# A two-layer conditioned trunk on one core: every engine's order computed in the kernel, and a first block in new rounds

## The chip, the core and the metric

The kernel runs on one core of one Trainium2 chip. A core has five engines that run side by side, each with its own queue of instructions that starts them in order: TensorE (PE in the profile; its weight loads are PEld) multiplies matrices, VectorE (DVE) and ScalarE (ACT) work on elements, GpSimd (POOL) does a few odd jobs, and SyncE (SP) issues most transfers. Data comes from device memory by DMA into the on-chip buffer SBUF; TensorE writes its results into PSUM, which has eight banks of 128 x 512 numbers. An engine waits for another by semaphores. The metric is the device time of one execution in microseconds (us), median of several runs.

## What is computed

One sequence of 256 positions, width 1024, two layers. Each layer is a half-step SwiGLU feed-forward, an attention, and another half-step feed-forward. Every sublayer first normalises x (RMS), then scales and shifts it with vectors that come from the condition c (adaLN), and multiplies its result by a gate that also comes from c:

```python
c_act = silu(c)
for layer in range(2):
    mods = c_act @ ada_w[layer] + ada_b[layer]
    sh1, sc1, g1, sh2, sc2, g2, sh3, sc3, g3 = split(mods, 9)
    h = rms_norm(x, norm_g[layer, 0]) * (1 + sc1) + sh1
    x = x + 0.5 * g1 * (silu(h @ w_gate) * (h @ w_up)) @ w_down
    ...
```

The attention of layer 0 ("MoBA") has 16 heads of 64, RMS-normalised q and k, a learned bias by bucketed distance, and a causal mask; with 256 positions it has a single block. Layer 1 ("MLA") projects x to small latents for q and for k and v, normalises, expands them to 16 heads, rotates a part of 32 (rope), and attends causally. All numbers are float32. 255 MB are read from device memory.

## The kernel before

**Products.** A float32 matrix is split into two parts of a shorter type, hi and lo (`split`: ScalarE copies to hi, VectorE subtracts to get lo, 128 x 1024 at a time). A product is then three matmuls, hi by hi, hi by lo and lo by hi (`mm3`, lines 394 to 396). Weights come in 0.5 to 1 MB transfers into a ring of three buffers (`rawp`, tile `raw`), in a fixed sequence (`wsrcs`, `wload`). A feed-forward makes a first block of 512 columns, then nine blocks of 256 columns of gate and up, then the down product.

**The adaLN vectors.** Eighteen vectors of 1024 are made beside the rest (`ada_vec`): eight slices of 128 x 1024 of ada_w come into a ring (tile `adaw`), and VectorE adds each, times c, to an accumulator (tile `acc`, line 211). The first step starts from a zeroed tile `bz` whose row 0 holds the bias, brought by a transfer from ScalarE's queue. TensorE then sums over partitions into a tile `adaps` (lines 222, 230 and 231).

**The first block.** It can't wait for the usual way. `first()` makes its shift and scale in four rounds of 256 columns: for each round two pairs of 0.5 MB transfers of ada_w and two of gate and up; VectorE's steps on 256 columns, shift and scale apart (`acc_step`); column sums on TensorE (`sums`, tile `at<-ones_r,acc`); `cols`; the modulated x (`shaped`, tile `z`); and then unsplit float32 products of z with the round's gate and up rows (`products`, tile `mm<-raw,z`; each is two records in the profile). Its order is written out by hand (`START`) and held by `in_turn` and `behind`, which queue each instruction behind the last of its engine. c comes as 1024 single numbers, one per element (`c_raw`).

**Side work.** The bias table of the MoBA attention is made during the first feed-forward (`bias_steps`: VectorE compares positions, tile `oh`, line 722; TensorE multiplies by table differences; ScalarE copies; the result goes to a DRAM tile `bias_d`). Rope tables and masks are made there too.

**Attention.** Per group of four heads: a projection into PSUM; square (line 698), sum (701), power on GpSimd (703) and scale give normalised q and k (`qn`, `kn`); TensorE transposes them (879, 1065); scores go into three PSUM banks (611); VectorE takes maxima, ScalarE exponentials (631), VectorE divides (637); TensorE transposes the probabilities (646) and multiplies by v (666). Between sublayers, x is normalised (`resid`, `stat`, `rstd_of`), transposed (442), modulated and split (`hh`, `hl`).

**Order.** Outside the first block the instructions are emitted by a clock of estimated matmul time: `later(us, fn)` emits fn when so much matmul work has been emitted, and a pace spreads the vectors. The tile scheduler then orders each engine's queue by this sequence. Transposes, scores and column sums share one ring of four PSUM banks (`ps_tr`); projections and products have the other four (`ps_mm`).

```python
ps_mm = ctx.enter_context(tc.tile_pool(name="ps_mm", bufs=4, space=PSUM))
ps_tr = ctx.enter_context(tc.tile_pool(name="ps_tr", bufs=4, space=PSUM))
```

Of the kernel before, what the change touches and what calls it, by code (L numbers as in the profile page):

```python
# [69 lines left out]


START = ("a10 a11 r0 a12 a13 y00 y01 q10 q11 y02 t00 y03 t01 a00 r1 b a01 a14 a02 y10 t02 a15 a03 "
         "y11 t03 y12 t10 y13 t11 t12 t13 a16 a04 a17 a05 a06 a07 s g").split()

BIAS_STEPS = [0, 0, 0, 3]
# [7 lines left out]
def bcast_row(ap, n, parts=P):  # L83
    return bass.AP(tensor=ap.tensor, offset=ap.offset, ap=[[0, parts], [1, n]])


@with_exitstack
def trunk(ctx: ExitStack, tc: tile.TileContext, a: dict, out: bass.AP):
# [11 lines left out]
    ps_tr = ctx.enter_context(tc.tile_pool(name="ps_tr", bufs=4, space=PSUM))  # L100
# [39 lines left out]
    def drain():  # L140
        while pend:
# [12 lines left out]
    bz = cp.tile([P, D], F32, name="bz")  # L154
    nc.vector.memset(bz, 0.0)
# [3 lines left out]
    c_raw = cp.tile([P, KD], F32, name="c_raw")  # L159
# [3 lines left out]
    nc.scalar.activation(cact, c_raw, AF.Silu)  # L163
# [10 lines left out]
    def split(src, n):  # L174
        hi = splitp.tile([P, n], F32R, tag="hi", name=nm("hi"))
        lo = splitp.tile([P, n], F32R, tag="lo", name=nm("lo"))
        in_turn(nc.scalar.activation, hi, src, AF.Copy, on="a")
        in_turn(nc.vector.tensor_tensor, lo, src, hi.bitcast(F32), op=ALU.subtract, on="v")
        return hi, lo

    chain = {}
    started = []

    @contextmanager
    def behind(*engines):

        with ExitStack() as es:
            for e in engines:
                if e in chain:
                    es.enter_context(tc.issue_after(chain[e].ins))  # L190
            yield

    def in_turn(fn, *args, on="p", **kw):

        if started:
            return fn(*args, **kw)  # L196
        with behind(on):
            chain[on] = fn(*args, **kw)  # L198
        return chain[on]

    def ada_vec(w, b, col, finish, rows):


        acc = adap.tile([P, D], F32, tag="acc", name=nm("acc"), bufs=1)
        nc.scalar.dma_start(bz[0:1, :], b[col:col + D].rearrange("(o n) -> o n", o=1))
        for k in range(KD):
            wt = adap.tile([P, D], F32, tag="adaw", name=nm("adaw"))
            with behind("s"):
                nc.sync.dma_start(wt, w[k * P:(k + 1) * P, col:col + D])
            with behind("v"):  # L210
                nc.vector.scalar_tensor_tensor(acc, wt, cact[:, k:k + 1], bz if k == 0 else acc,  # L211
                                               op0=ALU.mult, op1=ALU.add)
# [13 lines left out]
        def sums():  # L226
            for hh in range(2):
                pt = ps_tr.tile([P, 512], F32, tag="tr", name=nm("adaps"))
# [21 lines left out]
    def scale_col(ps, key, k0=0, n=KD):  # L250
        in_turn(nc.vector.scalar_tensor_tensor, col_slice(m_cols[:, 1, :], key, k0, n), ps, 1.0,
                col_slice(g_cols, key, k0, n), op0=ALU.add, op1=ALU.mult, on="v")
# [58 lines left out]
    def wsrcs():  # L311
        for layer in range(2):
            for idx in range(2):
                wg, wu, wd = (a[n][layer, idx] for n in ("ffn_w_gate", "ffn_w_up", "ffn_w_down"))
                if (layer, idx) == (0, 0):
                    for k0 in range(0, KD, 2):
                        yield [w[k0 * P:(k0 + 2) * P, :FB] for w in (wg, wu)], 4, FB
                else:
# [41 lines left out]
    def wload(src, kt, cols):  # L360
# [6 lines left out]
        for i, sr in enumerate(srcs):  # L367
            dst = rows[:, :, i * m:(i + 1) * m] if isinstance(src, tuple) else rows[:, i * n:(i + 1) * n, :]
            with behind("s"):
                ld = nc.sync.dma_start(dst, sr.rearrange("(k p) f -> p k f", p=P))  # L370
            if not started:
                chain["s"] = ld
# [35 lines left out]
    def split_evac(hi, lo, ps):  # L408
        in_turn(nc.scalar.activation, hi, ps, AF.Copy, on="a")
# [398 lines left out]
    def bias_step():  # L808

        if len(groups) < 2:  # L810
            next(side[0], None)
# [473 lines left out]
```

## Time and profile before

| | |
|---|---|
| median of 3 runs | 1063.77 us (1063.65 to 1065.18) |
| the profiled execution | 1067.16 us, span 1065.4 us |
| granted TensorE clock, mean | 0.998 |
| read from device memory | 255.33 MB, 244 GB/s over the span |
| instructions | 17278 |

The profile is one execution. Its span runs from the first to the last instruction on the core; "busy" is the time in which an engine has at least one instruction recorded as running, and the ends of matmuls are modelled. A group line names the line of the kernel, the engine, the operation, output and inputs with their shapes and the count, then busy time, the mean of one in ns, and the idle time of the engine ahead of it with what ended it. Many lines stand under a helper's line, so tiles are named where that matters.

### The profile page before, as it was taken

To read this page: it belongs to the slowest core of one execution; us is meant where nothing else is said; L and a number is where in the kernel's file an instruction comes from. 1 tells how busy PE (TensorE), PEld (TensorE's weight loads), DVE (VectorE), ACT (ScalarE), POOL (GpSimd) and SP (SyncE) were. 2 spreads that over 40 slices of the span, in tenths; PEclk is the share of its full clock that TensorE was granted. 3 is DMA by queue.
4 is the path that set the end of the run, shared out by engine and by line. 5 is a ranking of instruction groups with operands and counts; after the bars stand their busy time and mean duration, and the time that the engine had idled before them with its cause. 6 is when DMAs were issued, how large, how long until landed. Compare 5 with 4: busy or idle time off the path is not lost.

```text
span 1065.4 us, 17278 instructions
## 1 busy us (share of the span) xinstructions
PE 1020.8 (96%) x6663; PEld 899.3 (84%) x6663; DVE 810.9 (76%) x1244; ACT 578.6 (54%) x1048; POOL 70.1 (7%) x119
## 2 busy tenths in 40 slices
PE   4999999998999999999999999999988899999998
PEld 2499999886778789999887999988766778999986
DVE  5999977886875789889688888867778758755642
ACT  4364545357675765545348544533868777545531
POOL 4001000002121000000000000000043200000000
PEclk9999999999999999999999999999999999999999
DMA  9999987996845479989897997986354337665450
GB/s 311 322 304 287 376 288 278 335 318 206 310 162 170 139 236 345 337 293 332 295 313 227 328 329 251 318 303 205 117 162 142 119 119 236 223 204 187 161 177 20
DMA packets 166934, 260.65 MB, mean 245 GB/s; under 512 B 8030, under 2 KB 110214, under 8 KB 166852
## 3 DMA queue, kind: packets, MB, share of 16 engines
q1 hardware_dynamic: 164496, 254.70, 70.3%
q0 software_dynamic: 976, 3.37, 1.0%
q10 hardware_dynamic: 1380, 1.49, 0.5%
q8 instruction: 52, 0.85, 0.3%
q14 instruction: 30, 0.25, 0.1%
HBM read 255.33 MB, written 4.19 MB: 244 GB/s over the span
## 4 chain that ended last, share of the span: by engine, by line
PE 77%; DVE 10%; ACT 4%; DMA 4%; POOL 3%; issue 3%; SPq 0%; DVEq 0%; ACTq 0%; POOLq 0%
PE mm L394 23%; PE mm L396 23%; PE mm L395 23%; DVE lo L196 3%; POOL hr L703 3%; DMA adaw<-in_ada_w_dram 2%; PE mm L198 2%; ACT hi L196 1%; DVE oh L722 1%; PE adaps L222 1%; PE at L666 1%; PE at L611 1%; DVE acc L211 1%; DMA raw<-in_ffn_w_gate_dram 1%; ACT y L196 1%
## 5 line engine op out<-in xcount | busy, mean ns | idle before, releaser
L196 DVE TENSOR_TENSOR lo<-raw,hi 128x1024 fp32r<-128x1024 f32 (+2 forms) x316 | 374.3, 1199 | 80.2 <-ACT hi L196 79.3
L196 ACT ACTIVATE hi<-raw 128x1024 fp32r<-128x1024 f32 (+2 forms) x316 | 324.1, 1040 | 171.5 <-PE mm L396 103.6
L394 PE MATMUL mm<-hh,hi 128*128 128x256 f32 x1152 | 328.6, 285 | 0.0
L396 PE MATMUL mm<-hh,lo 128*128 128x256 f32 x1152 | 326.7, 284 | 0.5 <-DVE lo L196 0.5
L395 PE MATMUL mm<-hl,hi 128*128 128x256 f32 x1152 | 326.5, 283 | 0.0
L395 PEld LDWEIGHTS mm<-hl,hi 128*128 128x128 f32 x1152 | 221.7, 192 | 0.6 <-issue 0.2
L396 PEld LDWEIGHTS mm<-hh,lo 128*128 128x128 f32 x1152 | 221.6, 192 | 0.7 <-DVE lo L196 0.7
L394 PEld LDWEIGHTS mm<-hh,hi 128*128 128x128 f32 x1152 | 221.7, 192 | 0.6 <-issue 0.2
L211 DVE SCALAR_TENSOR_TENSOR acc<-adaw,cact,acc 128x1024 f32<-128x1024 f32 x126 | 162.8, 1292 | 20.6 <-DMA adaw<-in_ada_w_dram 16.2
L394 PE MATMUL mm<-hi,gh 128*128 128x512 f32 x352 | 138.0, 392 | 0.0
L395 PE MATMUL mm<-lo,gh 128*128 128x512 f32 x352 | 137.0, 389 | 0.0
L396 PE MATMUL mm<-hi,gl 128*128 128x512 f32 x352 | 137.0, 389 | 0.0
L394 PE MATMUL mm<-hi,hh 128*128 128x512 f32 (+1 forms) x240 | 96.7, 404 | 5.0 <-ACT hh L196 5.0
L396 PE MATMUL mm<-hi,hl 128*128 128x512 f32 (+1 forms) x240 | 94.0, 392 | 1.5 <-DVE hl L196 1.4
L395 PE MATMUL mm<-lo,hh 128*128 128x512 f32 (+1 forms) x240 | 93.4, 390 | 0.0
L560 ACT ACTIVATE g<-mm 128x256 f32<-128x256 f32 x72 | 27.3, 379 | 94.5 <-PE mm L396 94.5
L396 PEld LDWEIGHTS mm<-hi,gl 128*128 128x128 f32 x352 | 66.1, 188 | 13.8
L394 PEld LDWEIGHTS mm<-hi,gh 128*128 128x128 f32 x352 | 66.1, 188 | 13.2
L395 PEld LDWEIGHTS mm<-lo,gh 128*128 128x128 f32 x352 | 66.1, 188 | 13.1
L196 ACT ACTIVATE gh<-g 128x256 fp32r<-128x256 f32 x72 | 29.9, 416 | 69.6 <-DVE g L561 69.6
L394 PEld LDWEIGHTS mm<-hi,hh 128*128 128x128 f32 x240 | 45.1, 188 | 16.1 <-ACT hh L196 7.8
L396 PEld LDWEIGHTS mm<-hi,hl 128*128 128x128 f32 x240 | 45.1, 188 | 13.2 <-DVE hl L196 4.5
(222 smaller groups left out, 1114.8 us busy)
## 6 DMA issues: line engine op xcount, KB each, us to landing
adaw<-in_ada_w_dram SPq DMA_DIRECT2D x144, 512.0 KB, 6.8
raw<-in_ffn_w_gate_dram SPq DMA_DIRECT2D x42, 1024.0 KB, 7.3
raw<-in_ffn_w_up_dram SPq DMA_DIRECT2D x42, 1024.0 KB, 6.9
raw<-in_ffn_w_down_dram SPq DMA_DIRECT2D x40, 1024.0 KB, 6.6
raw<-in_moba_w_qkv_dram SPq DMA_DIRECT2D x16, 512.0 KB, 5.0
adaw<-in_kv_ada_w_dram SPq DMA_DIRECT2D x16, 512.0 KB, 5.6
raw<-in_ffn_w_down_dram SPq DMA_DIRECT2D x8, 512.0 KB, 3.6
raw<-in_moba_w_qkv_dram SPq DMA_DIRECT2D x4, 1024.0 KB
```

The lines of the kernel that those rows point to most:

```text
L196: return fn(*args, **kw)
L198: chain[on] = fn(*args, **kw)
L211: nc.vector.scalar_tensor_tensor(acc, wt, cact[:, k:k + 1], bz if k == 0 else acc, op0=ALU.mult, op1=ALU.add)
L222: nc.tensor.transpose(kslice(pt, j), kslice(acc, 4 * hh + j), ident)
L394: nc.tensor.matmul(ps, lh, rh, start=start, stop=False)
L395: nc.tensor.matmul(ps, lh, rl, start=False, stop=False)
L396: nc.tensor.matmul(ps, ll, rh, start=False, stop=stop)
L560: nc.scalar.activation(g, ps[:, 0], AF.Silu)
L611: nc.tensor.matmul(ps3[:, i, :], qTs(e, t), kTs(e, nk), start=bias is not None, stop=bias is not None or i == len(es) - 1)
L666: nc.tensor.matmul(po[i * DH:(i + 1) * DH, pr, t, :], vs(e, kb), pT[t, e, kb], start=kb == 0, stop=kb == t)
L703: nc.gpsimd.tensor_tensor(r, v2, mhalf[:, :nh], op=ALU.pow)
L722: return fn(*args, **kw)
```

## The change

**An order for every engine.** At the end of the kernel a new class reads all instructions emitted so far, works out who needs whom from the data each reads and writes, and from the rings of buffers, and places all instructions of the five engines in a modelled time. The model's durations are constants in the kernel. VectorE, ScalarE, GpSimd and SyncE take the ready instruction with the earliest latest time (`needs`); TensorE keeps the emitted order among those that are ready, but sums of adaLN vectors come first. This is repeated four times, each time with the last placement's times for TensorE, and the best is kept. Each engine's order is then chained, without semaphores: every instruction behind the one before it.

**The first block.** Five rounds of 128, 256, 256, 256 and 128 columns in place of four of 256. Shift and scale share an accumulator (512 columns a step); round 0 has no steps on VectorE, TensorE sums over ada_w itself (16 matmuls of one column). The hand-written order and its helpers are gone, and `wsrcs` leaves the first block's weights out.

**Smaller parts.** c comes as eight rows of 128, goes through Silu as rows, and is transposed by TensorE. An adaLN accumulator is zeroed by GpSimd, its row 0 is filled by a GpSimd transfer, and there are two of them; `bz` is gone. The column sums of the vectors get a PSUM bank of their own and the ring `ps_tr` has three. The bias steps and rope tables are not placed in the first 34 us.

```diff
+ROUNDS = (128, 256, 256, 256, 128)
+WAKE = 100.0
+SWITCH = 90.0
+RATE = 392.0
+FLIGHT = 8
+HELD = 34e3
+SOON = 300.0
+MARGIN = 400.0
+ROUND_OF_ORDER = 4
...
+def duration(i, aps):
...
+        elif dt == F32R:
+            c = max(256, cols) / 2.4 + 13.3
...
+class Order:
...
+    def needs(self, pe_time):
+        need = [1e12] * len(self.ins)
+        for k in range(len(self.ins) - 1, -1, -1):
+            then = [need[s] for s in self.succ[k]]
+            then += [need[self.uses[self.next_tile[t]][0]] for t in self.tiles_of[k] if t in self.next_tile]
+            d = min(then) - WAKE if then else 1e12
+            d -= 2200.0 + self.transfer(k) if self.dma[k] else self.cost[k][1]
+            if self.eng[k] == "PE":
+                d = min(d, pe_time[k])
+            need[k] = min([d] + [need[s] - 1.0 for s in self.after[k]])
...
+        def choose(e, t):
+            av = avail[e]
+            if e == "PE":
+                first = min(av)
+                old = [x for x in av if x[2] <= t - MARGIN]
+                x = min(old) if old else first
...
+            x = min(av)
+            for r, j in known[e]:
+                if r < t + min(self.cost[x[1]][0], SOON) and need[j] < x[0] - 500.0:
...
+    def apply(self):
+        info = mybir.DependencyInfo(mybir.DependencyClass.NoSync, mybir.DependencyReason.DATA)
+        for ks in self.work_out()[1].values():
+            for a, b in zip(ks, ks[1:]):
+                self.tc.add_manual_dep(self.ins[b], self.ins[a].name, info, reason="order")
...
-    ps_tr = ctx.enter_context(tc.tile_pool(name="ps_tr", bufs=4, space=PSUM))
+    ps_tr = ctx.enter_context(tc.tile_pool(name="ps_tr", bufs=3, space=PSUM))
+    ps_ada = ctx.enter_context(tc.tile_pool(name="ps_ada", bufs=1, space=PSUM))
...
-    nc.sync.dma_start(c_raw, a["c"].rearrange("o (k p) -> p (o k)", p=P),
-                      allow_slow_non_contiguous=True)
+    c_rows = tp.tile([P, 256], F32, tag="y", name="c_rows", bufs=4)[:KD, :P]
+    nc.sync.dma_start(c_rows, a["c"].rearrange("o (k p) -> (o k) p", p=P))
...
-        acc = adap.tile([P, D], F32, tag="acc", name=nm("acc"), bufs=1)
-        nc.scalar.dma_start(bz[0:1, :], b[col:col + D].rearrange("(o n) -> o n", o=1))
+        acc = adap.tile([P, D], F32, tag="acc", name=nm("acc"), bufs=2)
+        nc.gpsimd.memset(acc, 0.0)
+        nc.gpsimd.dma_start(acc[0:1, :], b[col:col + D].rearrange("(o n) -> o n", o=1))
...
-                pt = ps_tr.tile([P, 512], F32, tag="tr", name=nm("adaps"))
+                pt = ps_ada.tile([P, 512], F32, tag="ada", name=nm("adaps"))
...
     def bias_step():
 
         if len(groups) < 2:
-            next(side[0], None)
+            hold(lambda: next(side[0], None))
...
     def first():
...
+        nc.scalar.activation(c_rows, c_rows, AF.Silu)
+        pt = tr_tile()
+        nc.tensor.transpose(pt[:, :KD], c_rows, ident[:KD, :KD])
+        nc.vector.tensor_copy(cact, pt[:, :KD])
...
+        def load_ada(j):
+            c0, cw = starts[j], ROUNDS[j]
+            n = D // (2 * cw)
+            for k0 in range(0, KD, n):
+                t_ = splitp.tile([P, n, 2, cw], F32, tag="lo" if k0 // n % 2 else "hi", name=nm("adaw"))
+                for i in range(2):
+                    nc.sync.dma_start(t_[:, :, i, :], w[k0 * P:(k0 + n) * P, i * D + c0:i * D + c0 + cw]
+                                      .rearrange("(k p) f -> p k f", p=P))
...
+        def vectors(j):
+            cw, k0 = ROUNDS[j], starts[j] // P
+            n = cw // P
+            acc = adap.tile([P, 2, cw], F32, tag="acc", name=nm("acc"), bufs=2) if j else None
+            for k in range(KD if j else 0):
+                if k:
+                    nc.vector.scalar_tensor_tensor(acc, wt[j, k], cact[:, k:k + 1], acc,
+                                                   op0=ALU.mult, op1=ALU.add)
+                else:
+                    nc.vector.tensor_scalar(acc, wt[j, k], cact[:, :1], None, op0=ALU.mult)
+            pc = ps_ada.tile([P, 512], F32, tag="ada", name=nm("adaps"))
+            for i in range(2):
+                for m in range(n):
+                    for k in range(1 if j else KD):
+                        nc.tensor.matmul(pc[:, i * n + m:i * n + m + 1],
+                                         (acc if j else wt[j, k])[:, i, m * P:(m + 1) * P],
+                                         ones[:, 0:1] if j else cact[:, k:k + 1],
+                                         start=k == 0, stop=bool(j) or k == KD - 1)
...
+    Order(nc, tc, first_rank, held).apply()
```

In `needs`, `succ` are the instructions that need k's result, `next_tile` the tile that takes a buffer over when k's is free, and `after` the next tile of the same ring. `rank` gives the loads and rounds of the first block a time ahead of everything else. In `place` a transfer takes its turn on one shared rate (RATE, bytes per ns), SyncE may have eight in flight, and an engine may stay idle for up to 300 ns for a more urgent instruction that is about to be ready.

More of the change, by code (lines that the diff above doesn't have):

```diff
@@ L446, in fin @@
             modulate(pt, y, key, c0 // P, n)
-            chain["v"] = split_h(h, c0, n, y)
+            split_h(h, c0, n, y)
         due[0] = max(clock[0] + wait, due[0] + 0.01)
@@ L806, in bias_steps, with hold @@
             drain()
+    held = set()
+    def hold(fn):
+        n = len(nc.cur_bb.bb.instructions)
+        fn()
+        held.update(i.name for i in nc.cur_bb.bb.instructions[n:])
     def bias_step():
         if len(groups) < 2:
-            next(side[0], None)
+            hold(lambda: next(side[0], None))
         if groups:
@@ new lines, in first, with columns @@
+        for t in range(NT):
+            for hh in range(2):
+                stat(t, hh)
+            rs.append(rstd_of(t))
+        pt = tr_tile()
+        nc.tensor.transpose(pt[:, :NROW], g_rows[:NROW, :], ident[:NROW, :NROW])
+        nc.vector.tensor_copy(g_cols, pt[:, :NROW])
+        def columns(j):
+            c0, cw = starts[j], ROUNDS[j]
+            for t in range(NT):
+                y = tp.tile([P, 256], F32, tag="y", name=nm("y"), bufs=4)[:, :cw]
+                nc.scalar.activation(y, xs[t][:, c0:c0 + cw], AF.Copy, scale=rs[t])
+                pt = tr_tile()[:, :cw]
+                for k in range(cw // P):
+                    nc.tensor.transpose(kslice(pt, k), kslice(y, k), ident)
+                nc.scalar.activation(xT[t][:, c0:c0 + cw], pt, AF.Copy)
```

518 lines of the change are left out of this document (354 added, 164 removed).

## The prediction

> **What bounds the kernel now.** I read the page's busy times first, then a table of stages, then what TensorE waited for, then the timeline of the start.
>
> ```profile
> span 1065.4 us, 17278 instructions
> PE 1020.8 (96%) x6663; PEld 899.3 (84%) x6663; DVE 810.9 (76%) x1244; ACT 578.6 (54%) x1048; POOL 70.1 (7%) x119
> ```
>
> TensorE is the bound: it has no recorded work for only 1065.4 - 1020.8 = 44.6 us. The change takes no matrix work away, so what it can win lies in those 44.6 us and in small gaps inside "busy". The stages (start:end, length, busy PE, PEld, DVE, ACT, POOL, granted clock, DMA share, GB/s) say where they are:
>
> ```profile
> 0.00:20.00 20.00, 5.99 (x20) 3.18 (x21) 8.07 (x22) 9.85 (x26) 11.13 (x70) 1.00 0.93 293
> 20.00:40.00 20.00, 18.55 (x52) 9.53 (x53) 16.96 (x52) 6.44 (x18) 2.02 (x4) 1.00 1.07 382
> 40.00:54.00 14.00, 14.00 (x40) 6.77 (x39) 13.19 (x39) 5.69 (x12) 0.00 (x0) 1.00 0.79 248
> 54.00:120.00 66.00, 63.97 (x706) 61.41 (x706) 64.14 (x136) 36.59 (x90) 5.28 (x2) 0.97 0.94 314
> 120.00:240.00 120.00, 120.00 (x765) 109.02 (x763) 100.09 (x117) 58.50 (x79) 0.57 (x1) 1.00 0.89 312
> 240.00:380.00 140.00, 131.49 (x702) 106.18 (x702) 97.43 (x193) 97.00 (x208) 21.91 (x17) 1.00 0.57 192
> 560.00:580.00 20.00, 19.14 (x95) 15.57 (x93) 14.90 (x23) 16.56 (x38) 0.55 (x1) 1.00 0.68 212
> 740.00:880.00 140.00, 126.81 (x738) 102.45 (x737) 103.43 (x234) 101.68 (x251) 28.08 (x24) 1.00 0.43 135
> 880.00:1060.00 180.00, 180.00 (x1207) 166.83 (x1206) 104.62 (x118) 83.11 (x111) 0.00 (x0) 1.00 0.53 177
> ```
>
> Idle TensorE: 15.5 us in the first 40, 2.0 in 54 to 120 (where VectorE is busy 64.14 of 66), 8.5 in the MoBA attention (240 to 380), 0.9 around 560, 13.2 in the MLA attention (740 to 880). The feed-forward stages between have none: nothing can be won there. What ended the waits (engine, line, releaser: total, times, longest):
>
> ```profile
> PE tr L198 <- ACT y L198: 13.0, 3, 11.4
> PE mm L394 <- ACT hh L196: 5.0, 6, 1.2
> PE tr L879 <- DVE qn L858: 3.5, 3, 1.4
> PE tr L442 <- ACT y L437: 2.2, 3, 1.0
> PE tr L1065 <- DVE kn L1100: 2.1, 3, 1.0
> ```
>
> After the start they are many and short, each the end of a chain over ScalarE, VectorE and GpSimd: what an order of those engines decides.
>
> **The start, row by row.** The first block needs x (1.05 MB), 1024 x 2048 numbers of ada_w (8.39 MB) and 1024 x 512 of gate and of up (4.19 MB): 13.6 MB. The stage rows give 293 x 20 = 5.86 MB and 382 x 20 = 7.64 MB, 13.5 MB by 40 us. So today the data is there at 40, but TensorE's first block ends at 55.1 (the first split product starts there), because it began at 22.68:
>
> ```profile
> 22.68 6.31 PE L198 MATMUL mm<-raw,z 128*128 128x512 f32 x8 [1.45 <-ACT z L198]
> 28.83 0.95 PE L198 MATMUL at<-ones_r,acc 128*128 128x1 f32 x8
> 29.64 7.11 PE L198 MATMUL mm<-raw,z 128*128 128x512 f32 x16
> 55.14 0.68 PE L394 MATMUL mm<-hh,hi 128*128 128x256 f32 x1
> ```
>
> Each product is two records. Dense, 16 records take 7.0 us (7.11 less the overlap), 0.44 each; the first eight took 0.79 each.
>
> New rounds: 128, 256, 256, 256, 128 columns, each loading ada_w, then gate and up. I take 2.4 us until bytes flow, 5.86 / 17.6 = 333 GB/s up to 20 us and 382 GB/s behind, and 0.8 us for landing (a choice). The ada_w part of rounds 0 to 4 is then in at 9.5, 17.4, 26.0, 34.3 and 39.8 us, the weights at 11.1, 20.5, 28.8, 37.0, 41.1.
>
> ```profile
> L198 DVE SCALAR_TENSOR_TENSOR acc<-adaw,cact,acc 128x256 f32<-128x256 f32 x56 | 23.0, 478 | 0.4 <-DMA adaw<-in_ada_w_dram 0.3
> L211 DVE SCALAR_TENSOR_TENSOR acc<-adaw,cact,acc 128x1024 f32<-128x1024 f32 x126 | 162.8, 1292 | 20.6 <-DMA adaw<-in_ada_w_dram 16.2
> L198 ACT ACTIVATE z<-xT,m_cols 128x128 f32<-128x128 f32 x16 | 6.6, 483 | 20.5 <-DVE m_cols L198 20.5
> 29.81 0.16 DVE L198 TENSOR_TENSOR m_cols<-at,g_cols 128x2 f32<-128x2 f32 x1 [1.04 <-PE at L198]
> 30.27 1.65 ACT L198 ACTIVATE z<-xT,m_cols 128x128 f32<-128x128 f32 x4 [5.87 <-DVE m_cols L198]
> ```
>
> From a round's last ada_w byte to its first product: two steps of 512 columns (no row; between 478 ns at 256 and 1292 at 1024 the line gives 0.75 each) 1.5, column sums 0.95, three tiny VectorE steps 0.46 (29.81 to 30.27), one z 0.48: 3.4 us. Round 2 starts at 26.0 + 3.4 = 29.4 and with 7.0 + 0.95 ends at 37.3; round 3 starts at 37.7, ends at 45.2 with round 4's sums; round 4, half as long, ends at 48.7. Against 55.1 that is **-6.3 us**. Rounds 1 to 3 are paced by the DMA (8.3 us a round against 7.0 of products), so how early round 0 starts hardly matters. Bounds: -8.4 if only round 4 has to wait for its ada_w (39.8 + 3.4 + 3.5 = 46.7), 0 if the transfers run at 293 GB/s throughout (its 13.1 MB are then in at 2.4 + 44.7 + 0.8 = 47.9, and the block ends at 54.8).
>
> Then the next block's up weights: their buffer is round 3's, free at 45.2; behind gate and three 0.5 MB ada_w transfers (2.6 MB from 41.1 at 382 GB/s: 48) they land at 51.5, and the hi and lo copies follow.
>
> ```profile
> L196 DVE TENSOR_TENSOR lo<-raw,hi 128x1024 fp32r<-128x1024 f32 x300 | 361.5, 1220 | 75.5 <-ACT hi L196 74.7
> L196 ACT ACTIVATE hi<-raw 128x1024 fp32r<-128x1024 f32 x300 | 312.8, 1057 | 162.7 <-PE mm L396 96.3 <-PE mm L395 29.3 <-DMA raw<-in_ffn_w_down_dram 13.3
> ```
>
> 51.5 + 1.06 + 1.22 = 53.8. TensorE has 24 gate matmuls of 0.12 us and 8 transposes of 0.11 until 52.5, and in the new order little else is put there: **+1.0** (0 to +3).
>
> **c as rows, held side work.** The new c transfer, Silu, one transpose and a copy are done while ada_w is still coming, cover until 9.5 us; today's c lands 4.7 us after its issue (row below), so 0, and at most +1 if it lands as late. The bias and rope set-up is kept out of the first 34 us: 0, since TensorE's bias products start only behind the first block in both orders.
>
> **The adaLN vectors.** 18 bias rows leave ScalarE's queue and a zeroed tile; instead GpSimd zeroes an accumulator and issues the transfer, now with two accumulators.
>
> ```profile
> c_raw<-in_c_dram SPq DMA_DIRECT2D x1, 4.0 KB, 4.7
> L155 DVE MEMSET bz<- 128x1024 f32 x1 | 0.9, 912 | 0.2 <-issue 0.2
> L833 POOL MEMSET qz<- 64x512 f32 x1 | 0.5, 521 | 0.0
> g_rows<-in_ada_b_dram POOLq DMA_DIRECT2D x1, 8.0 KB, 5.3
> ```
>
> A 1024-column zeroing on GpSimd is not in the trace: 0.91 us on VectorE, twice the 512-column row gives 1.04; I take 1.04. With the transfer's 5.3 us it lies under the vector before (8 steps of 1.29 us). GpSimd is busy 70 us of 1065, and in the listing of the new order no zeroing stands among the attention's power steps: 0. Without that cover 18 x 6.3 us of the ada_w queue would be lost, and with it the weights behind it. The Trainium skill, page "SBUF — State Buffer", section "SBUF: two separate sides", says that VectorE and GpSimd exclude each other at a shared port for a whole instruction. By that rule the two zeroings in the VectorE-bound stretch would add 2 us; no run here shows it, and the sum leaves it out.
>
> **The fixed order.** The listing of both kernels' instructions shows the same products but other neighbours. I added up the matmuls that stand between a result and its transposes, at the spacing of dense stages: 256 columns 20 / 169 = 0.12 us, 512 columns 20 / 90 = 0.22.
>
> ```profile
> 900.00:920.00 20.00, 20.00 (x169) 20.00 (x168) 17.84 (x20) 10.54 (x15) 0.00 (x0) 1.00 0.82 291
> 1020.00:1040.00 20.00, 20.00 (x90) 16.57 (x89) 8.62 (x9) 6.13 (x6) 0.00 (x0) 1.00 0.39 137
> ```
>
> In MLA the thinnest covers were 2.8 us (group 0's k, and group 1's scores); now they are 5.4 and 3.6, and the others lie between 4.5 and 10 as before. I estimate the need at 5.5 us, the 4.3 of the MoBA chain below and one weight split of 1.22 in its way. Today's covers fall short of it by 2.7 + 2.7 + 1.0, the new ones by 1.9 + 0.9 + 0.1. That is 3.5 us. On VectorE and ScalarE the order is now by latest time, so the links of these chains no longer queue behind 1.2 us weight splits; I give it 1 us in MLA: **-4.5** of 13.2 (-10 to +8). In MoBA one cover grows (4.3 to 6.6 us) and the others stay at 6.1, where the chain over GpSimd still came late:
>
> ```profile
> L698 ACT ACTIVATE sq<-mm 128x512 f32<-128x512 f32 x8 | 4.8, 597 | 7.5 <-PE mm L396 7.4
> L701 DVE TENSOR_REDUCE hv<-sq 128x8 f32<-128x512 f32 x8 | 5.4, 681 | 2.2 <-ACT sq L698 2.2
> L703 POOL TENSOR_TENSOR hr<-hv,mhalf 128x8 f32<-128x8 f32 x8 | 16.8, 2101 | 55.6 <-DVE hv L702 55.6
> L858 DVE TENSOR_TENSOR qn<-mm,hr 128x512 f32<-128x512 f32 x8 | 5.5, 691 | 13.2 <-POOL hr L703 13.2
> ```
>
> Square, sum, power and scale are 0.60 + 0.68 + 2.10 + 0.69 = 4.1 us, 4.3 with the small step that adds EPS, so 6.1 is enough unless a link queues: most of the 3.5 us of that wait goes, **-3.0** of 8.5 (-7 to +5). In 54 to 120 VectorE's accumulations can now stand behind the splits, but the work stays: **-1.5** (-3 to +2). Around the norms **-0.5**.
>
> **Sum.** -6.3 + 1.0 - 1.5 - 3.0 - 0.5 - 4.5 = -14.8. The profiled execution took 1067.16 us (1.8 around its span), 3.4 above the median of 1063.77: 1052.4 on its own basis, **1049** against the median.
>
> **Rivals.**
> *Only the start gains.* Covers in attention are today mostly the same; if the engine queues don't matter, -5.3 is left: 1058.5.
> *Nearly all idle time goes.* -5.3 - 2.0 - 8.5 - 0.9 - 13.2 = -29.9: 1034. Against it: the norm chains (5.0 and 2.2 us above) are latency that no order removes.
> *Three banks instead of four (slower).* Transposes and scores share a ring that shrinks from 4 to 3 PSUM banks; the fourth serves adaLN sums alone, which MLA does not have. A group's scores take all three; the first is free after its maximum and its exponentials:
>
> ```profile
> L621 DVE TENSOR_REDUCE mx<-at 128x4 f32<-128x512 f32 x4 | 2.7, 682 | 0.0
> 818.31 1.41 ACT s L631 x8
> ```
>
> 0.68 + 1.41 = 2.1 us, in which no transpose can start. The new order puts 2.2 us of projections there: just enough. It decides if the projections' weights are late or ScalarE is taken: 8 groups x 2.1 = 17 us: 1066.
> *A cold first block (slower).* The first eight records took 0.79 us, not 0.44, after sparse work. If the waits between the DMA-paced rounds keep that pace, rounds 1 to 3 need 12.6 + 0.95 each from 20.8 and round 4 6.3: 67.7 in place of 48.7, 1068. The Trainium skill, page "TensorE: Matmul & The Clock Gate", section "Part 1: The HAM clock gate", says the array's clock is halved until a window of some 3.4 us was busy, and again after an idle one; the 0.79 against 0.44 agrees. By that rule gaps under 3.4 us do not bring it back, and mine are 1.3.
> *The order is fixed on wrong estimates.* An in-order queue then waits where the old order had other work, and that eats the gain: 1063. That the order does not take hold is out: the listing shows it.
>
> **How the numbers follow.** Forecast 0.47, start only 0.20, nearly all 0.13, wrong estimates 0.07, banks 0.08, cold 0.05. What a measurement here can tell from no change is 0.2%, 2.1 us: faster 0.80, same 0.07, slower 0.13. The range, 1034 to 1066, reaches from the case in which nearly all idle time goes to the edge of the banks case; left out are the cold case and what lies beyond those two.
>
> **What would show it.** Right: first split product near 49 to 50, DMA share about 1 until 41, a short wait for hi or lo near 53, idle of 5 to 6 us in MoBA and 8 to 9 in MLA. Wrong: the first split product after 53, records of 0.79 us behind round 0, waits of transposes on exponentials, or longer waits of TensorE on hi and lo in the feed-forward stages, which have none today.

## The result, and the profile after

The changed kernel takes 1095.1 us in the median (1093.33 to 1097.14), against 1064.47 us for the kernel before, measured beside it (1063.65 to 1065.26; the 1063.77 above is the median of the first three): slower, ratio 1.0288 (95% interval 1.0262 to 1.0314). 1049 had been forecast. The profiled execution took 1093.43 us, its span is 1091.7.

The page's busy times after:

```profile
span 1091.7 us, 17404 instructions
PE 1030.6 (94%) x6692; PEld 906.3 (83%) x6692; DVE 810.1 (74%) x1217; ACT 583.1 (53%) x1054; POOL 97.3 (9%) x155
```

TensorE's idle time grew from 44.6 to 61.1 us and its busy time by 9.8, of which 7.0 are round 0's column sums over ada_w, 16 matmuls of one column in 32 records. The table of stages after, same columns as before:

```profile
0.00:20.00 20.00, 13.05 (x46) 9.84 (x47) 6.44 (x18) 8.90 (x24) 9.50 (x52) 1.00 0.99 297
20.00:40.00 20.00, 18.77 (x69) 9.72 (x67) 15.24 (x33) 7.99 (x22) 0.40 (x1) 1.00 1.07 346
40.00:54.00 14.00, 11.90 (x28) 5.25 (x27) 9.41 (x26) 5.40 (x12) 5.93 (x25) 0.88 0.83 262
54.00:120.00 66.00, 59.15 (x661) 56.68 (x660) 62.09 (x120) 33.96 (x85) 6.52 (x4) 0.95 0.91 289
120.00:240.00 120.00, 113.30 (x748) 103.53 (x746) 104.32 (x138) 52.65 (x74) 5.77 (x8) 1.00 0.92 325
240.00:380.00 140.00, 133.34 (x710) 107.78 (x710) 110.69 (x202) 95.01 (x191) 25.72 (x19) 1.00 0.70 240
380.00:560.00 180.00, 170.56 (x1176) 157.99 (x1175) 145.07 (x165) 88.38 (x132) 10.73 (x15) 0.99 0.83 283
580.00:740.00 160.00, 152.36 (x1088) 141.26 (x1087) 114.67 (x138) 85.50 (x133) 6.27 (x6) 1.00 0.73 243
740.00:880.00 140.00, 133.01 (x748) 111.74 (x747) 108.90 (x228) 95.40 (x224) 23.91 (x22) 1.00 0.50 166
```

Two of the same windows before, which the prediction doesn't show:

```profile
380.00:560.00 180.00, 180.00 (x1222) 167.24 (x1222) 155.11 (x169) 88.08 (x121) 0.55 (x1) 1.00 0.91 316
580.00:740.00 160.00, 160.00 (x1128) 150.70 (x1128) 131.56 (x146) 75.09 (x101) 0.00 (x0) 1.00 0.84 290
```

The windows stand still while the stages behind them move, so the table only says where to look: the feed-forward windows (120 to 240, 380 to 560, 580 to 740), full before, now have 6.7, 9.4 and 7.6 us without matrix work. For lengths I cut the trace at the starts of products: a feed-forward runs from its first split product (lines 394 and 695, tile `hh`) to its last with `gl`. These lengths (us) are each kernel's one profiled execution; the right columns are experiments below.

| stage | before | after | sums later | landing +2 | both | round 0 on VectorE |
|---|---|---|---|---|---|---|
| to the first split product | 55.1 | 54.8 | 54.9 | 55.7 | 55.9 | 53.1 |
| rest of feed-forward 1 | 184.1 | 201.2 | 194.1 | 190.7 | 185.5 | 183.6 |
| MoBA, norm after it | 152.9 | 147.5 | 150.5 | 146.9 | 152.6 | 151.6 |
| feed-forward 2 | 169.5 | 185.3 | 174.6 | 177.3 | 170.0 | 170.1 |
| norm and feed-forward 3 | 193.6 | 200.0 | 195.7 | 192.4 | 196.3 | 196.2 |
| MLA | 140.6 | 133.5 | 131.7 | 134.6 | 135.6 | 134.1 |
| feed-forward 4 (no vectors) | 164.7 | 164.7 | 164.6 | 164.7 | 164.6 | 164.6 |

The attentions did get shorter, by 5.4 and 7.1 us. The first three feed-forwards lost 17.1, 15.8 and 6.4; between the same cuts TensorE has 32.7 us without work where it had 2.9. The fourth, in which no adaLN vector is made, lost nothing. What TensorE and VectorE waited for:

```profile
PE adaps L529 <- issue: 13.0, 7, 3.1
PE adaps L529 <- DVE m_cols L564: 5.2, 5, 2.6
PE adaps L529 <- DVE acc L518: 2.6, 1, 2.6
```

```profile
DVE acc L518 <- DMA adaw<-in_ada_w_dram: 34.8, 22, 4.5
DVE acc L518 <- DMA acc<-in_ada_b_dram: 7.6, 3, 4.3
DVE acc L518 <- DMA adaw<-in_kv_ada_w_dram: 5.6, 4, 2.3
```

20.8 us in front of column sums, where the view of before lists no such wait, and on VectorE 49.4 us for ada_w and bias rows (with 1.4 for the kv bias), 20.2 before:

```profile
DVE acc L211 <- DMA adaw<-in_ada_w_dram: 16.2, 12, 2.8
DVE acc L211 <- DMA adaw<-in_kv_ada_w_dram: 4.0, 3, 1.8
```

"issue" in TensorE's first row is a wait whose releaser the profile doesn't show; in the timeline VectorE's last step of the vector ends just ahead of it. One such place, VectorE's timeline and then TensorE's:

```profile
410.51 1.28 DVE L518 SCALAR_TENSOR_TENSOR acc<-adaw,cact,acc 128x1024 f32<-128x1024 f32 x1 [4.26 <-DMA acc<-in_ada_b_dram]
411.72 1.22 DVE L506 TENSOR_TENSOR lo<-raw,hi 128x1024 fp32r<-128x1024 f32 x1
412.85 0.68 DVE L564 TENSOR_REDUCE m_cols<-adaps 128x4 f32<-128x512 f32 x1
```

```profile
413.59 0.66 PE L529 MATMUL adaps<-ident,acc 128*128 128x128 f32 x4 [2.65 <-DVE m_cols L564]
```

A vector's first step is next in VectorE's queue, its bias row isn't there, and VectorE stands for 4.26 us with a split and the reduction of finished sums behind it. TensorE, whose own next instruction is the second half of those sums, stands too. Behind the first block no view shows a wait for a finished vector; it is the queues that make the lateness theirs.

The order also takes the vectors earlier: of VectorE's 144 steps, 51 and 52 fall into feed-forwards 1 and 2 (39 and 41 before) and 20 into the third (40). With the later landing below they are 47, 49 and 23 and most of the loss is gone, so that alone is not it.

### The profile page after: what moved, and what is told of

Read it like the earlier page. It is cut to its first block, busy times and chain, and to the rows that moved or that the text cites. A ratio compares the mean times of both kernels' runs of the same rounds, so it can differ in the third digit from the quotient of the medians.

```text
span 1091.7 us, 17404 instructions
## 1 busy us (share of the span) xinstructions
PE 1030.6 (94%) x6692; PEld 906.3 (83%) x6692; DVE 810.1 (74%) x1217; ACT 583.1 (53%) x1054; POOL 97.3 (9%) x155
## 4 chain that ended last, share of the span: by engine, by line
PE 58%; DVE 15%; DMA 12%; issue 11%; ACT 3%; POOL 1%; SPq 1%; DVEq 0%; ACTq 0%; POOLq 0%
PE mm L697 17%; PE mm L696 17%; PE mm L695 17%; DMA adaw<-in_ada_w_dram 6%; DVE lo L506 5%; DVE acc L518 4%; DMA raw<-in_ffn_w_gate_dram 1%; PE mm L1527 1%; PE at L911 1%; ACT hi L505 1%; DMA bias_d<-bt 1%; DMA acc<-in_ada_b_dram 1%; DVE oh L1091 1%; PE adaps L1496 1%; DMA adaw<-in_kv_ada_w_dram 1%
## 5 line engine op out<-in xcount | busy, mean ns | idle before, releaser
L518 DVE SCALAR_TENSOR_TENSOR acc<-adaw,cact,acc 128x1024 f32<-128x1024 f32 x144 | 184.1, 1279 | 50.2 <-DMA adaw<-in_ada_w_dram 34.8
L861 DVE TENSOR_TENSOR g<-mm,g 128x256 f32<-128x256 f32 x72 | 30.2, 419 | 45.7 <-ACT g L860 45.7
L513 POOL MEMSET acc<- 128x1024 f32 x18 | 17.2, 955 | 470.1 <-DVE lo L506 275.7
```

Source lines behind the costliest of these rows:

```text
L513: nc.gpsimd.memset(acc, 0.0)
L518: nc.vector.scalar_tensor_tensor(acc, wt, cact[:, k:k + 1], acc, op0=ALU.mult, op1=ALU.add)
L861: nc.vector.tensor_tensor(g, ps[:, 1], g, op=ALU.mult)
```

## The experiments

All are edits of the changed kernel, timed beside the kernel before. Two theories for the feed-forwards: the placement has VectorE's vectors ready too early (transfers placed sooner than they land), or the smaller parts cost (one bank for the sums, the GpSimd rows). For the start: VectorE's queue order, SyncE's waits, or the pace of the transfers.

**Sums later on TensorE (e2_sums_later).**

```diff
+            if self.eng[k] == "PE" and r > 6e4 and any(t.startswith("adaps") for t in self.tiles_of[k]):
+                r += 4000.0
```

> In the placement alone, TensorE may take the column sums of an adaLN vector only 4 us after they are ready by the model (behind 60 us); nothing else. Theory: the feed-forward stages lost 36 us because the sums stand first on TensorE at the very moment at which the model has their vector ready, so each lateness of VectorE or of a transfer is a wait of TensorE. Then the waits in front of the sums fall from 21 us to under 5, and the time to 1070 to 1080. Rival (VectorE and the transfers are late as a whole, and the sums only show it): the waits turn up at hi and lo and the time stays above 1088.

1073.69 us, 21.4 less, as expected; no wait in front of the vectors' sums is left, and VectorE's waits for ada_w and bias rows fell to 27.2 us. The margin matters. It is not yet the cause: a margin hides lateness whatever it comes from.

**One bank or four (e5_ring4).** `ps_ada` is gone, `ps_tr` has four banks, and all three `adaps` tiles come from it.

> The sums go back into the ring of transposes and scores, with four banks, as before; the bank of their own is gone; TensorE still takes them first, with no margin. If the missing margin is what costs, the first halves of the sums still wait for their vector and only the second halves, which wait for VectorE's reduction of the first (5.2 us), are better: 1085 to 1092. If the single bank is what costs, the waits in front of the sums go altogether: 1070 to 1078.

1095.52 us: no change (1095.1), and in neither of the two ranges. TensorE's waits in front of the sums:

```profile
PE adaps L528 <- issue: 16.1, 4, 6.3
```

The waits for the reduction are gone as expected, 5.2 us; the others stay, 16.1 us against 15.6, the longest 6.3 against 3.1. Neither the sums' single bank nor the ring of three sets this kernel's time. In the profile of the changed kernel itself, transposes waited for exponentials 0.3 us in all.

**Fewer fixed orders (e3_pe_as_emitted, e4_no_order).** In the first, the loop of `apply` skips TensorE; in the second, `Order(...).apply()` is left out.

> TensorE's order is not chained (the tile scheduler keeps the emitted sequence on it); VectorE, ScalarE, GpSimd and SyncE are chained as worked out. Theory (TensorE's fixed order with the sums first is what costs): no waits in front of the sums in the feed-forward stages; since the others are placed for another TensorE order, there are some waits at hi and lo in their place; 1065 to 1085. Rival (the orders of the other engines are what costs): 1090 or more, and the feed-forward stages stay 30 us longer than before.

> No engine is chained: all engines take the emitted sequence; the new rounds, the c rows, the GpSimd rows and the three and one PSUM banks stay. If the order is what costs in the feed-forward stages and what gains in the attentions, the feed-forward stages are within 2 us of before (165 to 184 us with the first block's rest) and the two attentions lose their 5.4 and 7.1 us again; the start, whose sequence by hand is gone, is worse than 54.8: 1065 to 1080. If the smaller parts cost (one bank for the sums, the bias rows through GpSimd), the waits in front of the sums stay and the time is above 1080.

1160.68 and 1101.97 us; both expectations missed. With TensorE alone unchained, the other engines serve an order that TensorE doesn't follow:

```profile
PE mm L698 <- DVE lo L508: 20.6, 15, 5.0
PE tr L745 <- ACT y L740: 20.2, 5, 10.6
```

So part of an order is worse here than none, and the run says nothing on the sums. With no order at all the first split product came at 62.5 (the sequence by hand is gone), MoBA took 163.8 and MLA 142.6 us: the attentions' gain does come from the order. The feed-forwards answer in two ways. The rest of the first took 184.1, as before: its loss is the order's. The second took 179.8 and norm and third 198.6, 10.3 and 5.0 more than before, so there part of the loss needs no order. In this kernel the single bank does cost, since the second half of a gate's sums waits in TensorE's queue for ScalarE's copy of the first:

```profile
PE adaps L537 <- ACT gate L575: 8.0, 3, 4.3
```

**Where the lateness comes from (e9_land2, e10_rate330, e11_land2_later4, e12_rate330_later4).** Only the placement's idea of a transfer changes: a later landing, or a lower shared rate. By the old constants a lone 512 KB transfer lands 1.4 + 524288 / 392e3 + 0.3 = 3.0 us after its issue; with the queueing that the placement adds, the expectation below gives 4.5 in the median. On the chip, first the kernel before, then the changed one:

```profile
adaw<-in_ada_w_dram SPq DMA_DIRECT2D x144, 512.0 KB, 6.8
```

```profile
adaw<-in_ada_w_dram SPq DMA_DIRECT2D x128, 512.0 KB, 6.2
raw<-in_ffn_w_up_dram SPq DMA_DIRECT2D x42, 1024.0 KB, 7.1
```

```diff
-                dur = dma_free + 300.0 - t
+                dur = dma_free + 2300.0 - t
```

```diff
-RATE = 392.0
+RATE = 330.0
```

> In the placement alone, each transfer lands 2 us later (the model's 512 KB transfers of ada_w land 4.5 us after their issue in the median, the trace has 6.5); the rate and the sums-first rule stay. Theory: the one root is that VectorE's fixed queue has steps of an adaLN vector ahead of work TensorE waits for, and they wait for transfers that the model has too early (49.4 us of such waits in the changed kernel, 20 before, 27 with the sums 4 us later). Then VectorE's waits for ada_w and its bias rows fall under 30 us, the waits of TensorE in front of the sums fall under 10 us, and the time is 1066 to 1078. Rival (the sums need a margin of their own on TensorE): VectorE waits less but TensorE still waits 15 us or more in front of the sums: 1084 or more.

> In the placement alone the shared transfer rate is 330 GB/s and not 392 (the stages of the changed kernel moved 240 to 346 GB/s). If transfers late by their rate are the root, VectorE's waits for ada_w fall under 30 us and the time is 1066 to 1080. If the lateness is the landing and not the rate, little changes: 1088 to 1098.

> Both: transfers land 2 us later in the placement, and the sums are taken 4 us after they are ready. If the two cover different lateness (transfers, and VectorE's own queue), this is better than each: 1060 to 1070, with under 20 us of VectorE's waits for ada_w. If they cover the same, it is as the 4 us run: 1070 to 1076.

> Both: 330 GB/s in the placement, and the sums 4 us later. If the rate is part of the cause, 1062 to 1070; if not, as the 4 us run: 1070 to 1076.

1068.94, 1069.42, 1066.36 and 1067.12 us, all in the ranges of their theories. Either constant alone takes back 26 of the 31 us. VectorE's and TensorE's waits with the later landing and nothing else:

```profile
DVE acc L518 <- DMA adaw<-in_ada_w_dram: 18.3, 18, 2.1
DVE acc L518 <- DMA adaw<-in_kv_ada_w_dram: 2.7, 3, 1.6
```

```profile
PE adaps L529 <- issue: 5.8, 6, 1.6
PE adaps L529 <- DVE acc L518: 1.2, 1, 1.2
PE adaps L529 <- DVE m_cols L564: 0.2, 1, 0.2
```

21.0 us where there were 49.4, and 7.2 where there were 20.8, with no margin given to the sums. So most of the loss comes from the transfers' time in the placement: two separate constants, each moved the later way, give back the same 26 us, while the edits of a fully ordered kernel that touch neither these constants nor the sums' margin (e1, e5, e6) ended between 1092 and 1105. Each moves a vector's steps back, by different waits: with the later landing no wait for a bias row is left (9.0 before it) and 21.0 for ada_w stay, with the lower rate 7.0 for bias rows and 7.4 for ada_w. Both at once were not run, so which constant is the wronger stays open. The margin on top is worth 2 to 3 us. With later landing and margin the ratio is 1.0003 (0.9985 to 1.0021): the time of before, not better.

**The start: the small loads (e1_held60, e6_consts100, e14_start_late_consts).** The side work let in at 34 us issues four small loads on ScalarE's queue, and SyncE stood behind one. SyncE's timeline and waits in the changed kernel:

```profile
33.73 8.17 SPq L1445 DMA_DIRECT2D adaw<-in_ada_w_dram  x4
```

```profile
SPq L1445 <- DMA gpek<-in_mla_k_g_dram: 5.6, 1, 5.6
```

In e1 HELD is 60e3; in e6 only `hold(rope_tables, 100e3)` and `hold(mla_consts, 100e3)` are later.

> HELD is 60 us in place of 34 us, nothing else. Theory: the first block lost its gain in its fourth round, because the side work let in at 34 us puts small element-wise loads on ScalarE's queue; SyncE's next ada_w issue waits for one of them for 5.6 us (34.9 to 41.0), round 4's ada_w comes late, and VectorE's first step of round 4 stands ahead of round 3's m_cols. Then the first split product comes at 49 to 51 us instead of 54.8, and the whole time falls by 3 to 5 us to 1090 to 1092. Rival (the rounds are slow by themselves, by VectorE's chain or a cold TensorE): the first split product stays at 53 or later and the time within 1 us of 1095. The column sums' waits in the feed-forward stages (some 21 us in all) stay in both.

> Only the rope tables and MLA's constants, with their small loads, are held until 100 us; the bias steps stay at 34 us. The kernel held to 60 us as a whole ended its first block at 52.6 instead of 54.8 but lost 4.7 us just behind it and more later. Theory: the gain comes from the small loads leaving SyncE's way, the loss from the bias steps being pushed into 60 to 130 us. Then this one has its first split product at 52 to 53, no 4.5 us wait at hi behind it, and the time is 1090 to 1094. Rival (the order worked out is so tight that any change moves the waits about): 1098 or more.

1104.63 and 1091.78 us. The first split product came at 52.6 in the one and at 55.2 in the other: e1 missed its range, and e6 met its time but not its start. So the small loads alone are not it: without them VectorE still stood at the same place, as its timeline in e6 shows:

```profile
41.99 0.35 DVE L1491 TENSOR_SCALAR acc<-adaw,cact 128x256 f32<-128x256 f32 x1 [1.85 <-DMA adaw<-in_ada_w_dram]
42.26 0.15 DVE L1500 TENSOR_TENSOR m_cols<-adaps,g_cols 128x2 f32<-128x2 f32 x1
```

Round 4's first step (L1491) waits for its ada_w, and round 3's finished sums (L1500), from which z is made, wait behind it. The whole of the side work moved to 60 us cost more behind the first block than it gained in it (54.3 us of VectorE's waits for ada_w and bias rows, the most of all runs).

**Margins and fragility (e7_later2_consts100, e8_later4_consts100).** As e6, with the sums 2 and 4 us later.

> As the one with constants at 100 us, and the sums 2 us after they are ready by the model, not 4. If 2 us cover most of VectorE's lateness, the waits in front of the sums are under 8 us and the gaps left by the 4 us hold get smaller: 1066 to 1074. If lateness is mostly over 2 us, the waits stay above 12 us: 1076 or more.

> As the one with constants at 100 us, and the sums 4 us later. If the two causes are separate, this is the 4 us run less 2 us: 1070 to 1073, with the first split product at 52 to 53. If they aren't, the gain of the start is taken back by waits in 55 to 130 us: 1074 or more.

1101.44 and 1072.04 us. With 2 us TensorE waited only 4.7 us in front of sums, as hoped, and the kernel was yet slower than with none: the order found this time had VectorE waiting 50.1 us for ada_w and bias rows, and TensorE waited for what stood behind. The 1072.04 lies in its range, but not for the reason given there: the first split product came at 56.7, not at 52 to 53, and e2, without that edit, took 1073.69. Over the runs the time goes with VectorE's waits: 49 to 54 us of them at 1095 to 1105, 39 to 41 at 1092 to 1096, 27 to 30 at 1072 to 1074, 11 to 21 at 1061 to 1069 (e3 and e4 aside, which don't fix every engine). Within the last group it doesn't: 21.0 at 1068.94, 14.4 at 1069.42.

**The start: VectorE's queue and round 0 (e13_start_late, e14_start_late_consts, e15_round0_vector, e16_all).** All have the landings 2 us later and the sums 4 us later; in the first 60 us the landings are 4 us later, which puts round 3's small steps ahead of round 4's first step. e14 also has e6's edit, e15 makes round 0 on VectorE like the others, e16 has both.

```diff
-            for k in range(KD if j else 0):
+            for k in range(KD):
...
-                    for k in range(1 if j else KD):
-                                         (acc if j else wt[j, k])[:, i, m * P:(m + 1) * P],
-                                         ones[:, 0:1] if j else cact[:, k:k + 1],
+                    for k in range(1):
+                                         acc[:, i, m * P:(m + 1) * P],
+                                         ones[:, 0:1],
```

> As the kernel with 2 us later landings and sums 4 us later, but in the first 60 us the placement lands transfers 4 us later. In that order VectorE's small steps of round 3 (m_cols) stand ahead of round 4's first ada_w step. If this queue order is what cost the start its gain, TensorE's 1 to 2 us wait for z and the slow records behind it go, and the first split product comes at 53 to 54 (55.9 without): 1062 to 1066. If the rounds are set by the transfers themselves, it stays at 55 or later and the time is that of the kernel without, about 1066.

> The same, and the small element-wise loads held until 100 us. If SyncE's wait of 5.6 us for one of them matters for the fourth round, this is 1 to 3 us better at the first split product than the one without; if the transfers are the limit there, no difference at the first split product (within 0.5 us).

> As the first of these three, with round 0 on VectorE like the other rounds (8 steps of 0.48 us and four column sums) in place of TensorE's 32 column sums over ada_w (7.0 us, 7.2 to 14.2). Round 1's steps on VectorE stood behind round 0's small steps until 15.0. If that is why the rounds start 2.7 us late, round 1's products start at 21 to 22 instead of 23.5, and the first split product is 1.5 to 3 us earlier. If the transfers set the pace, round 1 starts earlier but the first split product doesn't move by more than 0.5 us.

> Round 0 on VectorE, the small loads held until 100 us, landings 4 us later in the first 60 us and 2 us later behind, the sums 4 us later: all four edits of the runs before together. If VectorE's queue, SyncE's wait for the small loads and round 0 are separate delays of the start, the first split product comes at 50 to 52 and the time is 1057 to 1060, 0.4 to 0.7% below before. If the transfers set the pace of the rounds by now, the first split product stays at 53 and the time at about 1061.

| | median, us | ratio to before | first split product in its profile |
|---|---|---|---|
| e13 | 1063.50 | 0.9983 (0.9968 to 0.9998) | 57.6 |
| e14 | 1065.11 | 0.9989 (0.9975 to 1.0003) | 52.9 |
| e15 | 1060.89 | 0.9957 (0.9941 to 0.9974) | 53.1 |
| e16 | 1063.37 | 0.9979 (0.9963 to 0.9996) | 53.7 |

e13's time lies in its range by luck: the small steps do stand ahead, as meant, but the first split product came at 57.6 and not at 53 to 54, so that queue order is not shown to be what cost the start its gain. e15 is faster than both kernels, by 0.43% (0.26 to 0.59) against before. Round 0 on VectorE is what the runs show to help: 1060.89 against 1063.50 without, round 1's products at 21.99 in place of 24.30. The small loads show nothing in the times with it or without it; the 4.7 us between the first split products of e13 and e14 are two single executions, and the medians go the other way. e16 came out as its rival, 53.7 and not 50 to 52; why it is 2.5 us behind e15 was not settled. Also open is what the order by hand would do with the new rounds: not tried.

## Why the prediction was wrong

**The step that failed: "The feed-forward stages between have none: nothing can be won there."** I gave these stages no term, as if they could not lose either. An order that is fixed on every engine can lose exactly there: 17.1 + 15.8 + 6.4 us, most of it through waits of VectorE for transfers and of TensorE for sums. The rule that caused it stood in the change as I wrote it down ("sums of adaLN vectors come first", the durations as constants), and in the case of wrong estimates I priced it as eating the gain, 1063 at a chance of 0.07. Its price was not bounded by the gain. My sign for a loss in these stages was waits on hi and lo; they came in front of column sums. The first row to hold against it was in the profile before, the 6.8 us from issue to landing of ada_w, beside the constants' 3.0 for a lone transfer. What the runs put in its place: transfers later in the placement give back 26 of the 31 us, a margin for the sums 21, both all of it. What is not settled is the part that feed-forwards 2 and 3 lose with no order at all (10.3 and 5.0 us).

**The start (-6.3 forecast, -0.4 measured).** (55.1 - 48.7 is 6.4, a slip of no weight.) Three sizes were off. TensorE's timeline after:

```profile
7.19 6.96 PE L1496 MATMUL adaps<-cact,adaw 128*128 128x1 f32 x32 [3.56 <-DMA adaw<-in_ada_w_dram]
23.54 2.84 PE L1527 MATMUL mm<-raw,z 128*128 128x512 f32 x6 [1.10 <-ACT z L758]
42.61 5.40 PE L1527 MATMUL mm<-raw,z 128*128 128x512 f32 x8 [2.10 <-ACT z L758]
60.22 0.39 PE L695 MATMUL mm<-hh,hi 128*128 128x256 f32 x1 [1.70 <-ACT hi L505]
```

Round 0's column sums (16 matmuls, 32 records) had no term: they take 7.0 us, and VectorE's steps of round 1 queue behind round 0's small steps until 15.0, so round 1's products start at 23.5 and not at 20.8. I had written that it hardly matters how early round 0 starts, because the DMA paces the rounds; with e15 gaining from it, it does. Second, round 3 was to start at 37.7 and starts at 42.6, 2.1 us of it the wait for z behind VectorE's queue. Third, its first eight records then take 5.4 us and not 3.5: part of the cold rival, at one place behind round 0 instead of in every round. (The rounds' own waits for z, 1.10 us, and their transposes were in no term either.) The rates, 297 and 346 GB/s, were as assumed at first (293) and 9% lower then (382).

**The next block's up weights (+1.0):** right in mechanism, TensorE waited 1.70 us for hi (last row), which waited for them; near in size by luck, since hi could start at 59.1 instead of 51.5 and the block before it ended 6 us later too. **c as rows (0):** right, the first sums waited for ada_w, not for c. **Held side work (0):** SyncE's 5.6 us wait was not foreseen; no run shows that it cost time.

**The adaLN vectors (0).** The zeroing took 0.955 us where 1.04 was estimated, and cost nothing by itself. The bias row did: the cover that I named (the vector before, 8 steps of 1.29 us) assumes the transfer is issued with that vector's start, and where it was not, VectorE stood up to 4.3 us. In the place shown it was issued at 405.83: the zeroing had waited for an accumulator until 404.58, when the split of a finished vector freed it.

**54 to 120 (-1.5), norms (-0.5):** the first wrong in sign, +17.1 with the rest of feed-forward 1, and mostly with the same cause: 10.5 of it go with the later landing alone, 15.7 with the margin too. Around the norms nothing was won: TensorE's waits for y, hh and hl were 8.6 us and are 9.9.

**MoBA (-3.0) and MLA (-4.5):** right in mechanism and near in size: TensorE's time without work fell by 3.8 (8.5 to 4.7) and by 4.3 us (13.2 to 8.9). The stages got shorter by 5.4 and 7.1; some 1 us of MoBA's is a vector's eight records of sums that moved to other stages, while in MLA the records are the same and only their busy time is 2.7 us shorter. With the later landing alone both kept 6.0; with the margin too, MLA kept 5.0 to 6.5 and MoBA 0.3 to 1.3, while feed-forward 2 behind it fell from 177.3 to 170.0; 14 records of sums stand in MoBA then, against none.

**The rivals.** Three banks instead of four: out, by e5. Cold first block: seen once, above. That the kernel could end beyond 1068 was in no case.

## What to carry to other kernels

An order fixed on every engine can turn an error of its estimates into a wait of all engines behind it; before costing what it wins, compare its durations with the trace, the transfers' issue-to-landing times first. Place work that isn't needed for long with room for its lateness, and don't leave one engine out of the order: with TensorE left out it was 1161 us, with none fixed 1102. A stage that has no idle time can't win, but it can lose; give it a term.

## What was unexpected in the hardware

**GpSimd and VectorE at once.** The prediction cited the Trainium skill, page "SBUF — State Buffer", section "SBUF: two separate sides", by which the two exclude each other for whole instructions, and said that two zeroings would cost 2 us by it. The trace shows nothing of the kind for a zeroing; VectorE's timeline and GpSimd's:

```profile
530.78 2.35 DVE L506 TENSOR_TENSOR lo<-raw,hi 128x1024 fp32r<-128x1024 f32 x2
```

```profile
531.75 0.95 POOL L513 MEMSET acc<- 128x1024 f32 x1 [14.86 <-PE adaps L529]
```

It lies inside two back-to-back subtractions, which take 1.22 us each as they do without it. The exclusion does show elsewhere. The kernel before, GpSimd and then VectorE:

```profile
95.04 3.23 POOL L785 TENSOR_SCALAR_AFFINE_SELECT bt<-bt 128x2048 f32<-128x2048 f32 x1 [14.99 <-DMA adaw<-in_ada_w_dram]
```

```profile
96.32 3.02 DVE L211 SCALAR_TENSOR_TENSOR acc<-adaw,cact,acc 128x1024 f32<-128x1024 f32 x1
```

The step takes 1.28 us elsewhere; behind this select, which reads and writes SBUF, it takes 3.02 and ends 1.1 us after the select. In the changed kernel the same select (108.60 to 111.66) made a subtraction at 110.19 take 2.54 us. (A subtraction that began 0.14 us into the select before was not held; GpSimd's times are rough.) The section itself goes on to say that a VectorE operation with two SBUF inputs locks only against a GpSimd operation that reads SBUF, which a zeroing does not: read to its end it agrees with the trace, and the prediction, which left this condition out and took a zeroing for such an operation, misread it.

**The clock after waits.** Windows of 2 us, the granted clock in the third column from the end:

```profile
44.00:46.00 2.00, 2.00 (x4) 0.92 (x3) 0.74 (x2) 0.32 (x2) 0.00 (x0) 0.50 0.97 261
94.00:96.00 2.00, 2.00 (x17) 1.98 (x15) 2.00 (x12) 0.31 (x1) 0.00 (x0) 0.50 0.98 294
414.00:416.00 2.00, 2.00 (x19) 2.00 (x18) 2.00 (x3) 0.54 (x2) 1.39 (x2) 1.00 0.75 272
430.00:432.00 2.00, 2.00 (x11) 2.00 (x11) 2.00 (x4) 0.39 (x1) 0.00 (x0) 0.50 1.04 399
```

The clock was halved three times: behind the 2.1 us wait at 42.6, around two of 1.5 and 1.0 us that end at 90.2 and 92.9, and at one of 3.1 us that ends at 429.1. At the 2.65 us that end at 413.6, and at the 2.47 and 2.67 us that end at 102.9 and 723.3, it was not. A wait's length alone did not decide it, and that gaps under 3.4 us do not bring the low clock back, as the prediction had it, did not hold here: the 2.1 us did. Summed over the neighbouring windows, (1 - clock) x 2 us, the three lost 1.7, 3.4 and 1.7 us of clock, at most so much on top of the waits; one such place in the kernel before lost 1.7. The views print 1.00 also at the very start, where the traces hold no clock record yet: the first stands at 27.97 us before and at 19.20 after, and round 0's records, 1.06 us long ahead of it, are 0.59 us long behind it. So the prediction's slow first eight records were at the low clock, as it read them, and so were the first of round 0 in the changed kernel (six in 4.46 us from 15.89).
